# Two of the four weight sums of a seven-product quad made by a copying and an adding transfer on GpSimd's queue, and a sixth such quad in each pass of the ssm branch

## The chip, the cores and the metric

One core of a Trainium2 chip runs one launch of the kernel. The metric is the device time of that launch in microseconds. Timed runs of the kernel before gave 1389.09, 1389.74 and 1391.64, median 1389.74.

## The reference, cut to what matters

One layer of a hybrid block, on 256 rows of width 2048, all in float32: a normed input is projected into queries, keys, values, gates and the inputs of a state-space scan; attention and scan run beside each other; then

```python
merged = sigmoid(g_a) * (o_a @ w_attn_branch) + sigmoid(g_s) * (y @ w_ssm_branch)
x + merged @ w_out
```

and a last norm. The change lies in the product `y @ w_ssm_branch` (256 x 4096 by 4096 x 2048), and touches the products for the gate `g_a` and the values `v` (256 x 2048 by 2048 x 2048 each).

## The kernel before, in words

A float32 product is made of three products of TensorE in a faster format: every operand is split into a high part (ScalarE copies it with rounding, `hq`) and a low part (VectorE subtracts, `lq`), and high by high, high by low and low by high are added up in PSUM.

**Quads.** The branch, gate, value and output products run in passes over 1024 of the 2048 output columns (`quads`, called with `cc` 0 and 1). The unit of a pass is a quad: two blocks of 128 rows of the weight by two halves of 512 columns, so four pieces of 128 x 512, which `lay_quads` lays in DRAM in the order b12, b11, b22, b21 (first figure: the column half). The program holds one quad as two tiles `wq_0` (b12, b11) and `wq_1` (b22, b21), of 512 KB each. An ssm pass has 16 quads, a pass for `ga` or `v` has 8. A plain quad is eight products of a 128 x 128 block by a 128 x 512 piece, 24 matmuls. A quad named in `lefts` is done in seven products by Strassen's scheme (Winograd's form), 21 matmuls, but these need four sums of pieces of weights, and their splits: b11+b12 and b12+b22 (the two halves of the tile `t13`), then b11+b12+b22 and b11+b12+b22+b21 (the tile `t24`), each built on one before it. PE does the products in the order 1, 2, 3, 7, 5, 6, 4 (L786 to L792); 7 and 5 take the split of `t13`, 6 and 4 that of `t24`.

**Where the sums come from.** For `ga`, `v`, attention's branch and the output most seven-product quads have sums that were made earlier and stored in DRAM (`stored`), and load them as `tq`. Sums in line (the `elif seven` in `quad`, from L744) are made for five quads in each of the two ssm passes (1, 3, 5, 7, 9) and for quad 4 in each of the four `ga` and `v` passes: 14 quads, with four VectorE adds each (L751).

**Queues and order.** All weights are loaded by SyncE's queue (L724, L728). A loaded tile takes the next slot of a ring of six (`ring("w")`: four slots of the pool `stream`, two of `more`); its load waits until all readers of the slot's old tile are done. Rings of six also hold the `h` and `l` splits, which come free when PE has used them. `t13` and `t24` had a ring of two of their own (tag `T`). Splits and sums are issued with high priority, and `in_turn` keeps all splits and sums of weights in program order on VectorE. VectorE thus stands still if the next in that order isn't ready. `order` in the call of `quads` gives the order of the quads in a pass; in both ssm passes a seven-product quad stands beside a plain one through most of the pass. GpSimd has little to do: it clears small tiles and, at the start of ssm, makes `r_y` (L381).

Of the kernel before, what the change touches and what calls it, by code (L numbers as in the profile page):

```python
# [9 lines left out]
F32 = mybir.dt.float32  # L10
F32R = mybir.dt.float32r
AF = mybir.ActivationFunctionType
ALU = mybir.AluOpType
PSUM = bass.MemoryType.PSUM

P = 128
# [5 lines left out]
SH = 64  # L22
EPS = 1e-6
KT = D // P
UNIT = 1024
# [97 lines left out]
N_PK = 16 + 4 * 48 + 48 + 32 + 32 + 2  # L123
# [40 lines left out]
def hybrid_block(ctx: ExitStack, tc: tile.TileContext, wall, wq, xt, x, pk_d, cst_d, fw_d, out):  # L164
    nc = tc.nc
    ve, ac, gp, pe = nc.vector, nc.scalar, nc.gpsimd, nc.tensor

    lead = ctx.enter_context(tc.tile_pool(name="lead", bufs=1))
# [12 lines left out]
        return opened.enter_context(tc.tile_pool(name=name, bufs=2))  # L181


    pk = lead.tile([P, N_PK], F32, name="pk", tag="pk")
    half = lead.tile([P, 2], F32, name="half", tag="half")
    a_neg = lead.tile([SH, 1], F32, name="a_neg", tag="a_neg")
    cw = lead.tile([P, 240], F32, name="cw", tag="cw")
    small = lead.tile([P, 8], F32, name="small", tag="small")
    ones2, sums_x = small[:, 0:2], small[:, 2:4]
# [12 lines left out]
    def ring(tag, name):  # L202
        n = W_BUFS if tag == "w" else H_BUFS
        shape, dt = [P, UNIT], F32 if tag == "w" else F32R
        if more is not None:
            turns[tag] += 1
            turn = (turns[tag] - 1) % (n + MORE + (2 if tag == "w" and wide else 0))
            if turn >= n + MORE:
                return summed.tile(shape, dt, name=name, tag="T", bufs=2)
            if turn >= n:  # L210
                return more.tile(shape, dt, name=name, tag=tag, bufs=MORE)
        return stream.tile(shape, dt, name=name, tag=tag, bufs=n)
# [187 lines left out]
    yT0 = big.tile([P, KT, 2 * S], F32R, name="yT0", tag="yo0")  # L400
    yT1 = []
# [29 lines left out]
    def load_on(u):  # L431
        if u < 6:
            load(u + 4)
        if u < 3:
            nc.sync.dma_start(xr(2 * u + 10, 2 * u + 12), xt[:, 2 * u + 10 : 2 * u + 12, :])
        if u == 3:
            nc.sync.dma_start(pk[:, KT:], pk_d[:, KT:])
        if u == 6:

            for late in (th_s[:, 0, 0:1], cst[:, 0:1]):  # L440
                gp.tensor_copy(late, yT0[:, 13, 0:1].bitcast(F32))
            nc.sync.dma_start(th_s, x.rearrange("(i p) d -> p i d", p=P))
            nc.sync.dma_start(cst, cst_d[:, 768:])
# [275 lines left out]
    def quad(n, seven):  # L719
        ws, ts = [], []  # L720
        for j in range(2):
            ws.append(ring("w", f"wq{n}_{j}"))
            cut = 512 if j == 0 and n in stored else 0
            nc.sync.dma_start(ws[j][:, cut:], wq[n, :, j * UNIT + cut : (j + 1) * UNIT])  # L724
        if n in stored:
            for j in range(2):
                ts.append(ring("w", f"tq{n}_{j}"))
                nc.sync.dma_start(ts[j], stored[n][:, j * UNIT : (j + 1) * UNIT])  # L728
        parts = {}

        def halves(src, names, cut=0):
            h, l = ring("h", f"hq{n}_{names[1]}"), ring("l", f"lq{n}_{names[1]}")
            in_turn("h", ac.activation(h[:, cut:], src[:, cut:], AF.Copy))  # L733
            in_turn("l", ve.tensor_tensor(l[:, cut:], src[:, cut:], h[:, cut:].bitcast(F32), ALU.subtract))  # L734
            for j, name in enumerate(names):
                parts[name] = h[:, j * 512 : j * 512 + 512], l[:, j * 512 : j * 512 + 512]

        with tc.high_priority(L_AHEAD):
            halves(ws[0], ("12", "11"), 512 if seven else 0)
            halves(ws[1], ("22", "21"))  # L740
            if ts:
                halves(ts[0], (7, 5))
                halves(ts[1], (6, 4))
            elif seven:  # L744
                b12, b11, b22, b21 = (w[:, c : c + 512] for w in ws for c in (0, 512))
                t13, t24 = (summed.tile([P, UNIT], F32, name=f"t{n}_{e}", tag="T", bufs=2) for e in range(2))
                for t, a, b in (
                    (t13[:, :512], b12, b11), (t13[:, 512:], b12, b22),
                    (t24[:, :512], t13[:, :512], b22), (t24[:, 512:], t24[:, :512], b21),
                ):  # L750
                    in_turn("l", ve.tensor_tensor(t, a, b, ALU.add))  # L751
                halves(t13, (5, 7))
                halves(t24, (6, 4))
        return parts
# [62 lines left out]
    summed = ctx.enter_context(tc.tile_pool(name="summed", bufs=2))  # L817
# [6 lines left out]
    with tc.tile_pool(name="mid", bufs=2) as mid:  # L824
        def two(name):
            return [mid.tile([P, UNIT], F32, name=f"{name}_{e}", tag=f"s{e}", bufs=1) for e in range(2)]

        def norm_y():
            tot = bank("m2", 2, "tot_y")
            for i in range(2):  # L830
                for n in range(2):
                    pe.matmul(
                        tot[:, 2 * i : 2 * i + 2], ssq[:, n, i * P : (i + 1) * P], ones2,
                        start=(n == 0), stop=(n == 1),
                    )
            rsqrt_rows(tot[:, 0:4:2], INNER, "y")

        def scale_gs(cc, i):
            g, r = th_s[:, i, cc * 1024 : (cc + 1) * 1024], hrs[:, 1, i : i + 1]
            ac.activation(g, g, AF.Identity, scale=r, bias=r)  # L840

        sf = mid.tile([P, 5, 2, 3, P], F32R, name="sf_y", tag="sf", bufs=1)
        lefts = {}
        for m, n in enumerate((4, 1)):
            s6 = sf[:, 4 * m : 4 * m + n]
            h3, l3 = s6[:, :, 0], s6[:, :, 1]
            y = yT1[0] if m else yT0
            v = y.rearrange("p (n r) c -> p n r c", r=4)[:, :n, 2]
            h4, l4 = v[:, :, P:S], v[:, :, S + P :]
            left(lambda: two("left"), y, 0, n, h3, l3, h4, l4)  # L850
            for j in range(n):
                lefts[8 * m + 2 * j + 1] = [(h3[:, j, e], l3[:, j, e]) for e in range(3)] + [(h4[:, j], l4[:, j])]

        def gated(i, c, a, b, op):
            g = th_s[:, i, c * 512 : (c + 1) * 512]
            ve.tensor_tensor(b, a, b, op)
            ve.tensor_tensor(g, g, b, ALU.mult)

        def ssm_sums(cc):
            return [[t[:, c * 512 : (c + 1) * 512] for c in range(2)] for t in two(f"sums{cc}")]  # L860

        lefts_x = {}

        def left_x():
            sf = big.tile([P, 5, 2, 4, P], F32R, name="sf_x", tag="yo0")
            h4, l4 = sf[:, :, 0], sf[:, :, 1]
            for j0, n, r, o in ((0, 2, 2, 0), (2, 2, 2, 2), (2, 1, 0, 4)):
                h, l = h4[:, o : o + n], l4[:, o : o + n]
                left(lambda: two("left"), XT, j0, n, h[:, :, :3], l[:, :, :3], h[:, :, 3], l[:, :, 3], r)
            for j, u in enumerate((1, 3, 5, 7, 4)):  # L870
                lefts_x[u] = [(h4[:, j, e], l4[:, j, e]) for e in range(4)]

        for cc, order, then in (
            (0, (0, 2, 4, 6, 1, 8, 3, 10, 5, 12, 7, 11, 9, 13, 14, 15), {1: norm_y, 9: (0, 0), 11: (0, 1)}),
            (1, (1, 0, 3, 2, 5, 4, 7, 6, 8, 10, 11, 12, 9, 13, 14, 15), {2: (1, 0), 4: (1, 1), 7: left_x}),
        ):
            then = {n: f if callable(f) else lambda f=f: scale_gs(*f) for n, f in then.items()}
            quads(
                "ssm", cc, yT, 2 * KT, order, lefts, lambda: ssm_sums(cc), gated, then
            )  # L880

        th_a, vt = (
            [big.tile([P, D], F32, name=f"{n}{i}", tag=f"yo1{2 * e + i}") for i in range(2)]
            for e, n in enumerate(("th_a", "vt"))
        )
        lefts = lefts_x

        def gate(i, c, a, b, op):
            ve.tensor_tensor(b, a, b, op)
            ac.activation(b, b, AF.Tanh, scale=0.5)  # L890

        def value(i, c, a, b, op):
            ve.tensor_tensor(b, a, b, op)

        for tag, dst, finish in (("ga", th_a, gate), ("v", vt, value)):
            for cc in range(2):
                order = (0, 1, 3, 2, 4, 5, 7, 6)
                sums = [[dst[i][:, (2 * cc + c) * 512 : (2 * cc + c + 1) * 512] for c in range(2)] for i in range(2)]
                quads(tag, cc, lambda kt: XT[:, kt, :], KT, order, lefts, lambda: sums, finish)

    with tc.tile_pool(name="att", bufs=2) as ap, tc.tile_pool(name="ev2", bufs=2) as ev, tc.tile_pool(name="odd2", bufs=2) as odd:
# [46 lines left out]
        for h in range(NH):  # L948
# [5 lines left out]
            p = ap.tile([P, 384], F32, name=f"p{h}", tag="p", bufs=2)  # L954
# [11 lines left out]
    with tc.tile_pool(name="fin", bufs=2) as fp:  # L966
# [72 lines left out]
        lefts = empty()  # L1039
# [10 lines left out]
        lefts = empty()  # L1050
# [54 lines left out]
```

## Time and profile before

| what | value |
|---|---|
| timed runs, median | 1389.74 us |
| profiled execution | 1389.4 us |
| its span in the trace | 1387.6 us (1.8 us lie around it) |
| TensorE busy | 1374.8 us, 99% |
| VectorE busy | 1170.2 us, 84% |
| ScalarE busy | 830.5 us, 60% |
| GpSimd busy | 15.5 us, 1% |
| moved by DMA | 356.06 MB, 257 GB/s in the mean |
| ssm passes | 585.16 to 753.4 us |
| `ga` and `v` passes | 753.4 to 913.9 us |

A row of a timeline has the start, the duration, the engine, the line and the operation with its output and inputs; "x3" merges that many in a row. Matmul durations overlap, so what one costs is the step from start to start. The chain of waits is followed back from the last instruction and shows at each time what the rest waited for. "Issue to landing" of a DMA runs from its issue on the queue to its completion.

### The profile page before, as it was taken

The page shows a single profiled execution, that of the slowest core. Times are in us where ns is not written, and L with a number is a line of the kernel's source. Part 1 is how long each engine was busy: PE and PEld are TensorE (multiplying, and loading weights), DVE is VectorE, ACT ScalarE, POOL GpSimd, SP SyncE. Part 2 cuts the span into 40 slices and gives each one's busy share as a digit, 9 for nine tenths or more (in the row PEclk, how much of TensorE's full clock was granted, in tenths as well). Part 3 has the DMA queues.
Part 4 walks back from the last instruction along what each step waited for, and adds up shares of the span by engine and source line. Part 5 has one row for each costly group of instructions (what it writes and reads, how often), then busy time and mean ns, then how long its engine had stood idle before and what let it go on. Part 6 is the DMA issues. An engine that isn't in the chain of part 4 may idle for free.

```text
span 1387.6 us, 20439 instructions
## 1 busy us (share of the span) xinstructions
PE 1374.8 (99%) x7275; PEld 1170.2 (84%) x7275; DVE 1170.2 (84%) x1746; ACT 830.5 (60%) x1278; POOL 15.5 (1%) x70
## 2 busy tenths in 40 slices
PE   9999999999999999999999999999999999999997
PEld 7888888888888888888888888888888888878885
DVE  6988899887898888699997888887778776677997
ACT  6657767757566757465454667554544454464564
POOL 0000000000000000000000000000000000000010
PEclk9999999999999999999999999999999999999998
DMA  8678888798878775557576888898888887468765
GB/s 336 212 213 286 269 296 269 258 327 270 283 262 285 233 243 183 180 185 241 173 234 205 292 285 284 281 317 301 302 294 291 285 288 229 150 243 303 281 209 185
DMA packets 103110, 356.06 MB, mean 257 GB/s; under 512 B 11552, under 2 KB 12128, under 8 KB 102368
## 3 DMA queue, kind: packets, MB, share of 16 engines
q1 hardware_dynamic: 102432, 353.71, 75.9%
q8 instruction: 57, 0.93, 0.3%
q10 hardware_dynamic: 576, 1.05, 0.2%
q14 instruction: 45, 0.37, 0.1%
HBM read 322.14 MB, written 32.57 MB: 256 GB/s over the span
## 4 chain that ended last, share of the span: by engine, by line
PE 93%; DMA 3%; DVE 2%; ACT 1%; issue 1%; SPq 0%; POOL 0%; POOLq 0%; DVEq 0%; ACTq 0%
PE ps_xs L303 8%; PE ps_zs L303 8%; PE ps_xs L306 4%; PE ps_zs L306 4%; PE ps_q L303 4%; PE ps_k L303 4%; PE ps_za L303 4%; PE ps_ssm L771 4%; PE ps_ssm L772 4%; PE ps_ssm L773 4%; PE ps_k L306 2%; PE ps_za L306 2%; PE ps_q L306 2%; PE ps_gs L369 2%; PE ps_gs L368 2%; PE ps_gs L367 2%
## 5 line engine op out<-in xcount | busy, mean ns | idle before, releaser
L236 ACT ACTIVATE h<-w 128x1024 fp32r<-128x1024 f32 (+1 forms) x293 | 306.3, 1047 | 279.1 <-PE ps_za L303 47.5
L237 DVE TENSOR_TENSOR l<-w,h 128x1024 fp32r<-128x1024 f32 (+1 forms) x293 | 352.6, 1206 | 101.9 <-ACT h L236 99.1
L734 DVE TENSOR_TENSOR lq<-wq,hq 128x512 fp32r<-128x512 f32 (+1 forms) x192 | 206.6, 1100 | 43.6 <-ACT hq L733 42.5
L733 ACT ACTIVATE hq<-wq 128x512 fp32r<-128x512 f32 (+1 forms) x192 | 179.1, 959 | 105.6 <-PE ps_attn L773 16.2
L303 PE MATMUL ps_xs<-XT,h 128*128 128x512 f32 x496 | 176.3, 396 | 0.0
L303 PE MATMUL ps_zs<-XT,h 128*128 128x512 f32 x496 | 175.4, 395 | 0.0
L306 PE MATMUL ps_xs<-XT,l 128*128 128x256 f32 x496 | 139.7, 282 | 0.0
L306 PE MATMUL ps_zs<-XT,l 128*128 128x256 f32 x496 | 139.2, 281 | 0.0
L303 PEld LDWEIGHTS ps_xs<-XT,h 128*128 128x128 f32 x496 | 93.1, 188 | 21.1
L303 PEld LDWEIGHTS ps_zs<-XT,h 128*128 128x128 f32 x496 | 93.0, 187 | 21.1
L306 PEld LDWEIGHTS ps_xs<-XT,l 128*128 128x128 f32 x496 | 93.6, 189 | 0.8 <-issue 0.3
L306 PEld LDWEIGHTS ps_zs<-XT,l 128*128 128x128 f32 x496 | 93.6, 189 | 0.3
L303 PE MATMUL ps_q<-XT,h 128*128 128x512 f32 x256 | 90.6, 393 | 0.0
L303 PE MATMUL ps_za<-XT,h 128*128 128x512 f32 x256 | 89.7, 392 | 0.0
L303 PE MATMUL ps_k<-XT,h 128*128 128x512 f32 x256 | 89.7, 392 | 0.0
L772 PE MATMUL ps_ssm<-lq,yT 128*128 128x512 f32 x216 | 83.9, 389 | 0.0
L773 PE MATMUL ps_ssm<-hq,yT 128*128 128x512 f32 x216 | 83.7, 389 | 0.0
L733 ACT ACTIVATE hq<-tq 128x1024 fp32r<-128x1024 f32 x58 | 60.2, 1053 | 31.9 <-DMA tq<-sums_d 12.7
L734 DVE TENSOR_TENSOR lq<-tq,hq 128x1024 fp32r<-128x1024 f32 x58 | 69.2, 1218 | 11.9 <-ACT hq L733 11.9
L771 PE MATMUL ps_ssm<-hq,yT 128*128 128x512 f32 x216 | 77.1, 390 | 0.0
L306 PE MATMUL ps_q<-XT,l 128*128 128x256 f32 x256 | 74.4, 291 | 0.0
L306 PE MATMUL ps_k<-XT,l 128*128 128x256 f32 x256 | 71.7, 280 | 0.0
(325 smaller groups left out, 3001.9 us busy)
## 6 DMA issues: line engine op xcount, KB each, us to landing
w<-in_wall SPq DMA_DIRECT2D x288, 512.0 KB, 5.4
wq<-in_wq SPq DMA_DIRECT2D x163, 512.0 KB, 4.9
st<-in_wq SPq DMA_DIRECT2D x58, 512.0 KB, 5.1
sums_d<-st SPq DMA_DIRECT2D x58, 512.0 KB, 6.0
tq<-sums_d SPq DMA_DIRECT2D x58, 512.0 KB, 5.7
acb<-acum_d SPq DMA_DIRECT2D x32, 256.0 KB, 3.9
wq<-in_wq SPq DMA_DIRECT2D x29, 256.0 KB, 4.7
th_s<-in_x SPq DMA_DIRECT2D x1, 2048.0 KB, 10.0
```

The lines of the kernel that those rows point to most:

```text
L236: ac.activation(h[:, a:b], w[:, a:b], AF.Copy)
L237: last = ve.tensor_tensor(l[:, a:b], w[:, a:b], h[:, a:b].bitcast(F32), ALU.subtract)
L303: pe.matmul(acc[:width], h[:, kk, :], m, start=(kt == 0), stop=False)
L306: pe.matmul(acc[:width, S:], l[:, kk, :], m[:, :S], start=False, stop=(kt == n_kt - 1))
L367: pe.matmul(accs[i], xh, h, start=(kt == 0), stop=False)
L368: pe.matmul(accs[i], xh, l, start=False, stop=False)
L369: pe.matmul(accs[i], xl, h, start=False, stop=(kt == n_kt - 1))
L733: in_turn("h", ac.activation(h[:, cut:], src[:, cut:], AF.Copy))
L734: in_turn("l", ve.tensor_tensor(l[:, cut:], src[:, cut:], h[:, cut:].bitcast(F32), ALU.subtract))
L771: pe.matmul(accs[b], x[0], w[0], start=first, stop=False)
L772: pe.matmul(accs[b], x[0], w[1], start=False, stop=False)
L773: pe.matmul(accs[b], x[1], w[0], start=False, stop=stop)
```

## The change

In the branch without stored sums, `t13` is no longer made by VectorE. It takes a slot of the ring of six that the loaded weights use. GpSimd's queue first copies b12 from DRAM into both halves of it (one transfer of 512 KB written, 256 KB of DRAM read twice), and then adds b11 and b22 from DRAM onto it in a second transfer (512 KB). The second waits for the first. `t24` stays on VectorE with two adds; the first reads `t13` and b22, the second b21. All 16 quads with sums in line (there are 14 before) are made so.

In both ssm passes quad 11 becomes a seven-product quad, with its left factors made from the second of the `yT1` tiles; the order of the last quads is changed so that 9 and 11 stand between plain ones. To make room, the 64 numbers `a_neg` become a column of `pk`.

```diff
-    a_neg = lead.tile([SH, 1], F32, name="a_neg", tag="a_neg")
+    a_neg = pk[:SH, N_PK:]
...
-                b12, b11, b22, b21 = (w[:, c : c + 512] for w in ws for c in (0, 512))
-                t13, t24 = (summed.tile([P, UNIT], F32, name=f"t{n}_{e}", tag="T", bufs=2) for e in range(2))
+                b22, b21 = ws[1][:, :512], ws[1][:, 512:]
+                t13 = ring("w", f"t{n}_0")
+                gp.dma_start(
+                    t13.rearrange("p (a c) -> p a c", a=2), wq[n, :, :512].unsqueeze(1).to_broadcast([P, 2, 512])
+                )
+                gp.dma_start(t13, wq[n, :, 512 : 512 + UNIT], accum_op=ALU.add)
+                t24 = summed.tile([P, UNIT], F32, name=f"t{n}_1", tag="T", bufs=2)
                 for t, a, b in (
-                    (t13[:, :512], b12, b11), (t13[:, 512:], b12, b22),
                     (t24[:, :512], t13[:, :512], b22), (t24[:, 512:], t24[:, :512], b21),
                 ):
                     in_turn("l", ve.tensor_tensor(t, a, b, ALU.add))
...
-        sf = mid.tile([P, 5, 2, 3, P], F32R, name="sf_y", tag="sf", bufs=1)
+        sf = mid.tile([P, 6, 2, 3, P], F32R, name="sf_y", tag="sf", bufs=1)
...
-        for m, n in enumerate((4, 1)):
+        for m, (y, n) in enumerate(((yT0, 4), (yT1[0], 1), (yT1[1], 1))):
...
-            (0, (0, 2, 4, 6, 1, 8, 3, 10, 5, 12, 7, 11, 9, 13, 14, 15), {1: norm_y, 9: (0, 0), 11: (0, 1)}),
-            (1, (1, 0, 3, 2, 5, 4, 7, 6, 8, 10, 11, 12, 9, 13, 14, 15), {2: (1, 0), 4: (1, 1), 7: left_x}),
+            (0, (0, 2, 4, 6, 1, 8, 3, 10, 5, 12, 7, 13, 9, 14, 11, 15), {1: norm_y, 9: (0, 0), 11: (0, 1)}),
+            (1, (1, 0, 3, 2, 5, 4, 7, 6, 8, 10, 9, 12, 11, 13, 14, 15), {2: (1, 0), 4: (1, 1), 7: left_x}),
```

GpSimd's instructions at the start of the ssm passes, before (`raw_x` are the last cleared tiles of the scan, `r_y` is the norm's factor, `fs` belongs to the end of the kernel):

```order
L516 MEMSET raw_x_5913 128x4
L516 MEMSET raw_x_6042 128x4
L381 TENSOR_TENSOR r_y<-var_y,half 128x2
L1031 TENSOR_TENSOR fs<-fs 128x1
L1032 TENSOR_SCALAR fs<-fs 128x1
```

The same place now (`t_0_6539` is `t13` of the ssm pass's quad 1, `t_0_6626` that of quad 3):

```order
L516 MEMSET raw_x_6041 128x4
L747 DMA t_0_6539<-in_wq 128x2x512
L381 TENSOR_TENSOR r_y<-var_y,half 128x2
L750 DMA t_0_6539<-in_wq 128x1024
L747 DMA t_0_6626<-in_wq 128x2x512
L750 DMA t_0_6626<-in_wq 128x1024
```

A queue that was empty from `r_y` to the end now holds 32 transfers, in pairs; `r_y` stands between the first two.

VectorE in the first ssm pass, before: a plain quad (12), then a seven-product quad (7) with its four sums (`lq` are low parts, `t_0` is `t13`, `t_1` is `t24`):

```order
L734 TENSOR_TENSOR lq_11_6739<-wq_0_6734,hq_11_6738 128x1024
L734 TENSOR_TENSOR lq_21_6743<-wq_1_6736,hq_21_6742 128x1024
L734 TENSOR_TENSOR lq_11_6776<-wq_0_6771,hq_11_6775 128x512
L734 TENSOR_TENSOR lq_21_6780<-wq_1_6773,hq_21_6779 128x1024
L751 TENSOR_TENSOR t_0_6783<-wq_0_6771 128x512
L751 TENSOR_TENSOR t_0_6783<-wq_0_6771,wq_1_6773 128x512
L751 TENSOR_TENSOR t_1_6784<-t_0_6783,wq_1_6773 128x512
L751 TENSOR_TENSOR t_1_6784<-t_1_6784,wq_1_6773 128x512
L734 TENSOR_TENSOR lq_7_6790<-t_0_6783,hq_7_6789 128x1024
L734 TENSOR_TENSOR lq_4_6794<-t_1_6784,hq_4_6793 128x1024
```

The same two quads now:

```order
L734 TENSOR_TENSOR lq_11_6749<-wq_0_6744,hq_11_6748 128x1024
L734 TENSOR_TENSOR lq_21_6753<-wq_1_6746,hq_21_6752 128x1024
L734 TENSOR_TENSOR lq_11_6786<-wq_0_6781,hq_11_6785 128x512
L734 TENSOR_TENSOR lq_21_6790<-wq_1_6783,hq_21_6789 128x1024
L755 TENSOR_TENSOR t_1_6796<-t_0_6793,wq_1_6783 128x512
L755 TENSOR_TENSOR t_1_6796<-t_1_6796,wq_1_6783 128x512
L734 TENSOR_TENSOR lq_7_6800<-t_0_6793,hq_7_6799 128x1024
L734 TENSOR_TENSOR lq_4_6804<-t_1_6796,hq_4_6803 128x1024
```

Two of the four sums are gone from VectorE; the first of the two that stay reads what GpSimd's transfers have written.

More of the change, by code (lines that the diff above doesn't have):

```diff
@@ L181, in pool @@
         return opened.enter_context(tc.tile_pool(name=name, bufs=2))
-    pk = lead.tile([P, N_PK], F32, name="pk", tag="pk")
+    pk = lead.tile([P, N_PK + 1], F32, name="pk", tag="pk")
     half = lead.tile([P, 2], F32, name="half", tag="half")
-    a_neg = lead.tile([SH, 1], F32, name="a_neg", tag="a_neg")
+    a_neg = pk[:SH, N_PK:]
     cw = lead.tile([P, 240], F32, name="cw", tag="cw")
@@ L436, in load_on @@
         if u == 3:
-            nc.sync.dma_start(pk[:, KT:], pk_d[:, KT:])
+            nc.sync.dma_start(pk[:, KT:N_PK], pk_d[:, KT:])
         if u == 6:
@@ L840, in scale_gs @@
             ac.activation(g, g, AF.Identity, scale=r, bias=r)
-        sf = mid.tile([P, 5, 2, 3, P], F32R, name="sf_y", tag="sf", bufs=1)
+        sf = mid.tile([P, 6, 2, 3, P], F32R, name="sf_y", tag="sf", bufs=1)
         lefts = {}
-        for m, n in enumerate((4, 1)):
-            s6 = sf[:, 4 * m : 4 * m + n]
+        for m, (y, n) in enumerate(((yT0, 4), (yT1[0], 1), (yT1[1], 1))):
+            s6 = sf[:, 3 + m : 4 + m] if m else sf[:, :4]
             h3, l3 = s6[:, :, 0], s6[:, :, 1]
-            y = yT1[0] if m else yT0
             v = y.rearrange("p (n r) c -> p n r c", r=4)[:, :n, 2]
@@ L851, in hybrid_block @@
             for j in range(n):
-                lefts[8 * m + 2 * j + 1] = [(h3[:, j, e], l3[:, j, e]) for e in range(3)] + [(h4[:, j], l4[:, j])]
+                lefts[2 * (3 + m if m else j) + 1] = [(h3[:, j, e], l3[:, j, e]) for e in range(3)] + [(h4[:, j], l4[:, j])]
         def gated(i, c, a, b, op):
```

## The prediction

> **What bounds the kernel now.** I read the page's first part, then who waited for whom on PE, then busy time by stage.
>
> ```profile
> span 1387.6 us, 20439 instructions
> PE 1374.8 (99%) x7275; PEld 1170.2 (84%) x7275; DVE 1170.2 (84%) x1746; ACT 830.5 (60%) x1278; POOL 15.5 (1%) x70
> ...
> PE warm L418 <- POOL ssq L415: 1.4, 1, 1.4
> PE ps_first L327 <- ACT h L236: 1.2, 2, 1.0
> PE ps_attn L771 <- ACT hq L733: 0.4, 1, 0.4
> PE ps_v L771 <- ACT hq L733: 0.2, 1, 0.2
> ```
>
> TensorE is the bound. Its four waits in the whole kernel add up to 3.2 us, and only the last, 0.2 us, lies in what the change touches. So there is hardly a stall to win; time goes down only with the number of matmuls, and goes up as soon as something is late for PE. By stage (ssm passes, then `ga` and `v`; the columns used are PE, DVE, and at the end clock, DMA share and GB/s):
>
> ```profile
> 585.16:753.40 168.24, 168.24 (x746) 139.41 (x747) 154.13 (x200) 93.43 (x109) 1.61 (x1) 1.00 0.63 205
> 753.40:913.90 160.50, 160.34 (x708) 132.49 (x707) 138.02 (x148) 105.11 (x116) 0.00 (x0) 1.00 0.84 287
> ...
> 610.00:651.00 41.00, 41.00 (x182) 33.91 (x181) 39.99 (x50) 25.25 (x29) 0.00 (x0) 1.00 0.65 207
> ```
>
> In ssm PE is never idle and the granted clock is 1.00, but VectorE is close behind: 154 of 168 us, and 39.99 of 41 us where seven-product and plain quads alternate. DMA has room there (0.63, 205 GB/s) and less in `ga` and `v` (0.84, 287 GB/s).
>
> **Part 1: the sixth seven-product quad.** The chain of waits shows what a matmul costs when PE runs through:
>
> ```profile
> 690.62 0.45 PE ps_ssm L771 x2
> 692.43 0.91 PE ps_ssm L771 x4
> ```
>
> 0.91 / 4 = 0.227 us. Two quads (one a pass) go from 24 matmuls to 21: 6 x 0.227 = **-1.36 us**, all on the path, since PE has no idle time there. A plain quad then takes 24 x 0.227 = 5.44 us on PE, one of seven products 4.76, a pair of both 10.2. The added splits and left factors go to ScalarE (93 of 168 us busy) and VectorE.
>
> **Part 2: VectorE's load.** The sums before, one quad of the first pass, and the splits between two quads' sums:
>
> ```profile
> 625.61 0.68 DVE L751 TENSOR_TENSOR t<-wq 128x512 f32<-128x512 f32 x1
> 626.21 0.68 DVE L751 TENSOR_TENSOR t<-wq,wq 128x512 f32<-128x512 f32 x1
> 626.82 1.41 DVE L751 TENSOR_TENSOR t<-t,wq 128x512 f32<-128x512 f32 x2
> 628.14 2.52 DVE L734 TENSOR_TENSOR lq<-t,hq 128x1024 fp32r<-128x1024 f32 x2
> 630.58 4.09 DVE L734 TENSOR_TENSOR lq<-wq,hq 128x1024 fp32r<-128x1024 f32 x4
> 634.58 0.68 DVE L751 TENSOR_TENSOR t<-wq 128x512 f32<-128x512 f32 x1
> ```
>
> A pair takes 634.58 - 625.61 = 8.97 us of VectorE. The two adds that go are the first two rows, 626.82 - 625.61 = 1.21 us, so a pair takes 7.8 us, against PE's 10.2. For the two new quads VectorE does, against a plain quad, two more splits and two adds less half a split, 2.4 + 1.3 - 0.5 = 3.2 us, and some 1.5 us of left factors; the ten older ones give back 12.1. Net about -3 us on VectorE in ssm: no loss, and no gain either, since PE never waited for it.
>
> **Part 3: the two transfers, on which all hangs.** `t13` is now late or in time by GpSimd's queue. In a run of pairs five slots are taken by each pair, and the slot that `t13` of one seven-product quad takes is six places back: the tile `wq_1` of the seven-product quad before. That is read last by the second add of that quad's `t24`. So from one `t24` to the next lies one chain: end of the add, copy (D1), adding transfer (D2), two adds (1.3 us by the step of the row "x2" above), and signals between them (0.15, a guess from the 0.05 us steps of "issue" in the chain below). With D = D1 + D2, the period is L = D + 1.45. PE needs one quad every 10.2 us. While VectorE waits for `t13`, its later splits wait too, by `in_turn`.
>
> How much may L exceed 10.2? The first seven-product quad:
>
> ```profile
> 605.53 0.68 DVE L751 TENSOR_TENSOR t<-t,wq 128x512 f32<-128x512 f32 x1
> ...
> 609.97 0.62 PE L771 MATMUL ps_ssm<-hq,sf_y 128*128 128x512 f32 x2
> ...
> 598.47 1.61 POOL L381 TENSOR_TENSOR r_y<-var_y,half 128x2 f32<-128x2 f32 x1 [50.03 <-DVE var_y L379]
> ```
>
> PE came to product 7 at 609.97. Its low part is used 0.23 us later and takes VectorE about 1.0 after the sums, so they must be done by 609.2. They were, at 606.2. Now D2 is queued behind `r_y` on GpSimd, which ends at 600.1; with 4.5 to 6 us and two adds the sums end at 605.9 to 607.4. The lead at the start is thus 1.8 to 3.3 us; I take 2.5. Ten such quads follow each other without a break (1, 3, 5, 7, 9, 11 and, in the second pass, 1, 3, 5, 7), so nine periods: no stall if 9 x (L - 10.2) < 2.5, that is L < 10.48, **D < 9.0 us**. Above that every 1 us of D costs 9 us.
>
> No transfer on GpSimd's queue, and none that adds, is in the trace. The nearest rows are SyncE's 512 KB loads, first in the ssm passes:
>
> ```profile
> L724 SPq DMA_DIRECT2D wq<-in_wq x63: 327/328/425, 584.8 to 745.6; - x63
> ...
> DMA to landing us min/median/max: 3.4/4.5/6.9
> ...
> wq<-in_wq SPq DMA_DIRECT2D x2, 256.0 KB, 4.0
> ...
> wq<-in_wq SPq DMA_DIRECT2D x44, 512.0 KB, 5.5
> tq<-sums_d SPq DMA_DIRECT2D x28, 512.0 KB, 5.8
> ```
>
> The first four rows are of the ssm passes, the last two of `ga` and `v`. Two transfers in series: 6.8 us by the least, 9.0 by the median, 13.8 by the most. I take D1 = 4.0 (only 256 KB come out of DRAM, and nothing stands before it in its own queue, where SyncE's loads come in twos) and D2 = 4.5 to 5.0 (it reads its target as well): D = 8.5 to 9.0, just at the bound. Stall 0 at 8.5.
>
> The Trainium skill, in "DMA: Bandwidth & Descriptors", section "Anatomy of one DMA — SWDGE (gpsimd) path", fits 2.0 us plus bytes over 436 GB/s for a transfer of that queue: 3.2 us for 512 KB as an estimate, 6.4 for both. By that the sum is -1.36 with 2.6 us to spare; no run here shows a transfer of that kind yet, and by the rows above there is nearly nothing to spare.
>
> **Part 4: the four `ga` and `v` passes.** They get the transfers too, one pair a pass. The last pass is the tight one; the chain of waits there:
>
> ```profile
> 881.82 6.03 DMA wq<-in_wq
> 887.91 0.05 issue
> 887.96 1.07 ACT hq L733
> 889.05 1.23 DVE lq L734
> 890.27 1.82 DVE t L751 x3
> 892.12 0.70 DVE t L751
> ...
> 895.88 8.11 DMA tq<-sums_d
> 904.09 1.07 ACT hq L733
> 905.20 0.73 PE ps_v L771 x2
> ```
>
> It runs from a slot that comes free at 881.8 through quad 4's load and its sums to the next load and PE's 0.2 us wait. `t13` would take the slot of quad 3's first stored sum, whose split ends one split later, about 882.9. With D = 8.5 it has landed at 891.5, VectorE's two adds end at 892.8, as now. Each us more of D is a us of stall there. The `a_neg` column, the two new left factors' ScalarE work (at 56% busy) and `r_y`, whose readers come quads later, I cost at nothing: none stands before a matmul that waits.
>
> **The sum.** -1.36 us at D up to 8.5. The profiled execution took 1389.4, so 1388.0; on the median of the runs, 1389.74, it is **1388.4 us**. A change of 0.2%, 2.8 us, is about what a measurement of this kernel can tell from none, so this is no change that can be told.
>
> **The rivals.**
>
> A. *The chain over `t13` becomes the bound* (slower). Mechanism: D above 9.0, so PE waits in each of the pairs after the lead is used. For it: the ssm passes get 12 x 1.05 MB more over 168 us, 75 GB/s, so 280 in all, nearly the 287 at which the loads of `ga` and `v` take 5.5 us. Two of those are 11.0: L = 12.45, stall 9 x 2.25 - 2.5 = 17.8 us, time 1389.7 - 1.4 + 17.8 = 1406. With D = 10.3 (one at 4.5, one at 5.8) it is L = 11.75, 11.4 us, 1399.8. Against it: those 5.5 us hold waiting behind up to three other loads of the same queue, which GpSimd's does not have. It is slower by 0.2% from D = 9.5 on (L = 10.95, 9 x 0.75 - 2.5 = 4.3, less 1.36). The skill's section "Issuing engines are not separate DMA queues" on the same page says that transfers of all queues run on the same 16 engines and interleave; by it the added 75 GB/s would lengthen all loads and this rival is the likelier one.
>
> B. *ssm keeps up, the last `v` pass doesn't.* At 5.5 us each D = 11.0 there, the adds end at 882.9 + 11.0 + 1.45 = 895.4, 2.6 us later than now: 1391.0. The three passes before have about 1 us more lead, so little more comes from them. Still within 0.2%.
>
> C. *VectorE's relief brings more than the matmuls*, faster. It would need idle time of PE to remove; there is 0.2 us in these stages. To pass 2.8 us, over 1.4 would have to come from elsewhere, and I see no place.
>
> D. *The change doesn't do what it says*: the sixth quads save nothing since their factors or sums are late. The left factors are made in the first four quads, 22 us ahead of PE's first use; what is late then is A at a small D. 1389.7 to 1391.
>
> **How the numbers follow.** Forecast 0.38, B 0.09, D 0.04: no change, 0.51. A: 0.47, since D's rows reach from 6.8 to 13.8 around a bound of 9.0. C: 0.02. The likeliest one's own range is 1387.6 to 1389.7. The range asked for must go into A: to 1407, past its 5.5-us-loads case, which leaves about 0.1 above; at the lower end 1387.2, -1.36 with another 1.2 us, leaves 0.04.
>
> **What would show it.** Right: 738 matmuls on `ps_ssm` become 732, still at 0.227; no wait of PE in the ssm passes; on VectorE the step from one quad's first `t24` add to the next stays 10.2 us or less; D1 + D2 below 9.0 from issue to landing. A: that step is 11 us and more, VectorE idle before the first `t24` add with the transfer as releaser, and PE waiting for ScalarE's `hq` in pairs from about the third seven-product quad on. B: the first wait of PE in the last `v` pass. Wrong altogether: transfers of under 7 us for both and still a loss, which would mean contention on other loads, not the chain.

## The result, and the profile after

The changed kernel takes **1491.68 us** in the median of four runs (1487.79 to 1494.25), against 1390.07 us for four runs of the kernel before beside it: a ratio of 1.0727, 95% interval 1.0715 to 1.0740. It is about 100 us slower. The forecast was 1388.4 with a range to 1407, so both were wrong; of the rivals it is A, at several times its price.

The first part of the page, then PE's waits (total us, times, longest):

```profile
span 1486.0 us, 20553 instructions
...
PE 1414.6 (95%) x7269; PEld 1190.1 (80%) x7269; DVE 1161.1 (78%) x1733; ACT 831.5 (56%) x1284; POOL 41.6 (3%) x102
...
PEclk9999999999999999978899999999999999999999
...
DMA t<-in_wq 10%; PE ps_xs L303 8%; PE ps_zs L303 8%; PE ps_xs L306 4%; PE ps_zs L306 4%; PE ps_q L303 4%; PE ps_za L303 4%; PE ps_k L303 4%; DMA tq<-sums_d 2%; PE ps_k L306 2%; PE ps_za L306 2%; PE ps_q L306 2%; PE ps_gs L369 2%; PE ps_gs 
```

```profile
PE ps_ssm L775 <- ACT hq L733: 41.5, 20, 5.3
PE ps_v L775 <- ACT hq L733: 8.6, 5, 3.9
PE ps_ga L775 <- ACT hq L733: 7.3, 4, 3.0
```

PE has the six matmuls less that were forecast (7275 before, 7269 now). But PE, which had 0.2 us of waits in these stages, now has 57. The releaser named is ScalarE's `hq`; ScalarE is not the cause, since the same page has the transfers into `t13` (`t<-in_wq`) as the first item of the chain that ended last, and in its groups ScalarE and VectorE both wait for them:

```profile
L733 ACT ACTIVATE hq<-t 128x1024 fp32r<-128x1024 f32 x32 | 33.8, 1058 | 156.4 <-DMA t<-in_wq 146.0
L755 DVE TENSOR_TENSOR t<-t,wq 128x512 f32<-128x512 f32 x32 | 22.1, 691 | 115.9 <-DMA t<-in_wq 115.5
```

By stage (ssm, the two `ga` passes, the two `v` passes; PE, PEld, DVE, ACT, POOL busy, granted clock, DMA share, GB/s):

```profile
585.00:825.00 240.00, 197.00 (x740) 152.75 (x741) 149.98 (x195) 96.59 (x115) 21.29 (x25) 0.86 0.68 195
825.00:916.30 91.30, 84.02 (x348) 67.85 (x347) 64.87 (x69) 50.94 (x58) 3.22 (x4) 0.94 0.80 265
916.30:1012.40 96.10, 87.54 (x365) 70.39 (x364) 68.04 (x74) 52.91 (x60) 3.21 (x4) 0.95 0.83 277
```

The ssm passes went from 168.2 to 240.0 us (+72), `ga` and `v` together from 160.5 to 187.4 (+27). That is the whole difference of the spans, 98.4 us. The ssm stage moves fewer GB/s than before (195 against 205), though its DMA engines are busy a larger share of it (0.68 against 0.63). That this is not a lack of bandwidth is shown further on, by number 9, which moves 250 GB/s in the same stage without loss.

One period of the chain of waits in ssm, from one first `t24` add to the next (start, us, what; "issue" at 648.07 is the copy on its way, which the chain doesn't name):

```profile
645.23 0.70 DVE t L755
645.93 0.03 issue
645.96 0.70 DVE t L755
646.65 0.03 POOLq L747
646.69 0.65 issue
647.34 0.73 POOL t L747
648.07 5.34 issue
653.41 0.01 POOLq L747
653.42 8.46 DMA t<-in_wq
661.88 0.03 issue
661.91 0.02 DVEq L755
661.93 0.04 issue
661.98 0.70 DVE t L755
```

There is no PE in it, so PE doesn't set this pace. Two adds 1.4, 0.7 from the last add to the copy's issue, copy 6.1, adding transfer 8.5, 0.1 to the next add: 16.75 us. PE needs a quad of this kind every 10.2. The two transfers over the whole kernel, copy first:

```profile
DMA to landing us min/median/max: 4.6/6.2/8.0
DMA to landing us min/median/max: 6.5/7.6/9.2
```

VectorE's `t24` adds of the first, the fourth and the tenth seven-product quad:

```profile
610.92 1.42 DVE L755 TENSOR_TENSOR t<-t,wq 128x512 f32<-128x512 f32 x2 [6.62 <-DMA t<-in_wq]
661.98 1.42 DVE L755 TENSOR_TENSOR t<-t,wq 128x512 f32<-128x512 f32 x2 [8.90 <-DMA t<-in_wq]
762.76 1.42 DVE L755 TENSOR_TENSOR t<-t,wq 128x512 f32<-128x512 f32 x2 [8.11 <-DMA t<-in_wq]
```

(762.76 - 610.92) / 9 = 16.87 us a period, and each time VectorE stands idle 6.6 to 8.9 us for the transfer.

### The profile page after: what moved, and what is told of

It reads as the page before. It is cut to its first block, busy times and chain, and to the rows that moved or that the text cites. A ratio compares the mean times of both kernels' runs of the same rounds, so it can differ in the third digit from the quotient of the medians.

```text
span 1486.0 us, 20553 instructions
## 1 busy us (share of the span) xinstructions
PE 1414.6 (95%) x7269; PEld 1190.1 (80%) x7269; DVE 1161.1 (78%) x1733; ACT 831.5 (56%) x1284; POOL 41.6 (3%) x102
## 4 chain that ended last, share of the span: by engine, by line
PE 74%; DMA 13%; issue 7%; DVE 3%; ACT 1%; POOL 1%; SPq 0%; POOLq 0%; DVEq 0%; ACTq 0%
DMA t<-in_wq 10%; PE ps_xs L303 8%; PE ps_zs L303 8%; PE ps_xs L306 4%; PE ps_zs L306 4%; PE ps_q L303 4%; PE ps_za L303 4%; PE ps_k L303 4%; DMA tq<-sums_d 2%; PE ps_k L306 2%; PE ps_za L306 2%; PE ps_q L306 2%; PE ps_gs L369 2%; PE ps_gs L368 2%; PE ps_gs L367 2%
## 5 line engine op out<-in xcount | busy, mean ns | idle before, releaser
L733 ACT ACTIVATE hq<-t 128x1024 fp32r<-128x1024 f32 x32 | 33.8, 1058 | 156.4 <-DMA t<-in_wq 146.0
L755 DVE TENSOR_TENSOR t<-t,wq 128x512 f32<-128x512 f32 x32 | 22.1, 691 | 115.9 <-DMA t<-in_wq 115.5
L734 DVE TENSOR_TENSOR lq<-tq,hq 128x1024 fp32r<-128x1024 f32 x58 | 69.6, 1222 | 12.9 <-ACT hq L733 12.8
```

## The experiments

The theory: *the chain*. `t13` takes a slot that the quad before gives back only after its `t24` adds, so both transfers lie in series between one quad's adds and the next's. Its rivals: *traffic*, the transfers make all loads slower; *the sixth quads*, whose work VectorE or ScalarE can't carry; *the adding* itself, being slow; and *the ring*, in which `t13` takes one of the six slots that the loads had. Each ratio is against runs of the kernel before on the same chip.

**1. The sixth quads alone.** The changed kernel with the four VectorE sums of before:

```diff
-                t13 = ring("w", f"t{n}_0")
-                gp.dma_start(
...
-                gp.dma_start(t13, wq[n, :, 512 : 512 + UNIT], accum_op=ALU.add)
...
+                t13, t24 = (summed.tile([P, UNIT], F32, name=f"t{n}_{e}", tag="T", bufs=2) for e in range(2))
+                    (t13[:, :512], b12, b11), (t13[:, 512:], b12, b22),
```

> The sixth seven-product quad alone: all four sums on VectorE as before, no transfer on GpSimd's queue. Theory (the chain copy, adding transfer, sums, slot makes the whole loss): two quads save 6 x 0.227 = 1.36 us and VectorE's 8.97 us a pair stay under TensorE's 10.2, so 1388.7 us, within 1387.5 to 1390. Rival (the sixth quad costs by itself, by VectorE or by a worse order of the last quads): 1393 to 1420.

Measured 1393.64, ratio 1.003 (1.0021 to 1.0039): 4 us slower, the rival's number. After the new quad VectorE (the third busy time) has hardly a gap, and PE has a wait that the kernel before doesn't have, for an `hq` that stands behind VectorE's sums:

```profile
672.00:712.00 40.00, 37.75 (x160) 30.59 (x159) 39.78 (x49) 20.51 (x23) 0.00 (x0) 0.96 0.54 173
```

```profile
PE ps_ssm L771 <- ACT hq L733: 2.8, 2, 2.3
```

The sixth quads explain 4 of the 100 us. But VectorE's relief is not worthless, as I had it: without it the sixth quad costs more than its matmuls save. (The new order and the left factors are not what costs: number 4 has them too, with two VectorE adds a quad less, and loses nothing.)

**2. The transfers alone.** The kernel before, five quads a pass, with the changed branch for `t13`:

```diff
-                t13, t24 = (summed.tile([P, UNIT], F32, name=f"t{n}_{e}", tag="T", bufs=2) for e in range(2))
+                t13 = ring("w", f"t{n}_0")
+                gp.dma_start(
...
+                gp.dma_start(t13, wq[n, :, 512 : 512 + UNIT], accum_op=ALU.add)
...
-                    (t13[:, :512], b12, b11), (t13[:, 512:], b12, b22),
```

> The transfers alone: five seven-product quads a pass as before, t13 made by copy and adding transfer. Chain theory: a period of 16.9 us against TensorE's 10.2, but the run of quads is broken by three plain quads (13, 14, 15) between the passes, where 21 us pass between two seven-product quads: 4 x 6.7 - 2.5 = 24 us in the first pass, 3 x 6.7 - 4 = 16 in the second, and about 25 in the ga and v passes as after: near 1455 us. Rival (traffic on the 16 DMA engines): the loss goes with the number of transfers, 28 of 32, +88 us, 1478. Rival (the sixth quads): back to 1390.

Measured 1469.23, 1.0573 (1.0559 to 1.0587). The transfers are the cause, sixth quads are not needed for it. The number lies between chain and traffic (1455 and 1478) and doesn't separate them. The trace does: the `t24` adds of the five quads of the first pass go from 611.93 to 680.34, (680.34 - 611.93) / 4 = 17.1 us a period, each after an idle time of VectorE that ends with the transfer.

**3. The slot taken earlier.** `t13` takes its slot and starts its transfers ahead of its own quad's loads:

```diff
+        if seven and n not in stored:
+            t13 = ring("w", f"t{n}_0")
+            gp.dma_start(
...
+            gp.dma_start(t13, wq[n, :, 512 : 512 + UNIT], accum_op=ALU.add)
...
             elif seven:
-                t13 = ring("w", f"t{n}_0")
-                gp.dma_start(
...
-                gp.dma_start(t13, wq[n, :, 512 : 512 + UNIT], accum_op=ALU.add)
```

> As the changed kernel, but t13 takes its slot of the ring ahead of the quad's two loads, and both transfers are issued there. Same bytes, same transfers, same number of slots. Its slot then is that of the plain quad before the seven-product quad in front, so the chain closes over two pairs only: 15.2 of transfers + 1.3 of adds + 4.2 of splits = 20.7 us for 20.4 of TensorE. Chain theory: the ssm passes lose 0 to 8 us instead of 72, the ga and v passes about 3 us less each than after: 1395 to 1420 us. Rival (traffic on the DMA engines, or too few slots for the loads): as after, 1480 to 1495.

Measured 1437.55, 1.0346 (1.0332 to 1.0360), outside both ranges. The same bytes and transfers cost half as much when only the place of the slot and of the issue changes: this speaks for the chain and against traffic. The `t24` adds of the first seven seven-product quads go from 606.91 to 683.93, (683.93 - 606.91) / 6 = 12.8 us a period, still above 10.2. Now the loads are late too (ScalarE's waits for `wq` are 62.1 us, 12.1 in the kernel before):

```profile
ACT hq L739 <- DMA wq<-in_wq: 62.1, 43, 6.9
ACT hq L739 <- DMA t<-in_wq: 38.1, 10, 5.5
```

A slot held from the start of the copy to the last read is missing for the loads. So it seems to be not only which slot `t13` gets, but also how long one of the loads' six is held; this is read from the waits, no run varies it by itself.

**4. The copy alone.**

```diff
-                gp.dma_start(t13, wq[n, :, 512 : 512 + UNIT], accum_op=ALU.add)
```

> As the changed kernel without the adding transfer (t13 holds b12 twice, so the sums are not those of the reference). Chain theory: period 0.7 + 6.1 + 1.5 = 8.3 us, below 10.2, so no stall in ssm and next to none in ga and v: 1388 to 1392 us. Rival (traffic): half the added bytes are left, half the loss, about 1440 us.

Measured 1391.37, 1.0007 (0.9998 to 1.0016): the loss is gone, with the slot's place as in the changed kernel and half of D. The copies take 4.7 / 7.2 / 8.0 us (least, median, most), so L is about 7.2 + 2.2 = 9.4, below 10.2. PE's waits on `ps_ssm` are 0.7 us, the stage takes 168.6 us (168.2 before):

```profile
584.70:753.30 168.60, 167.86 (x743) 138.22 (x741) 149.60 (x196) 97.51 (x115) 10.57 (x13) 1.00 0.73 242
```

`t13` still takes one of the six slots here, and the slot is still the shared one. So neither the ring with a slot less nor the shared slot costs anything by itself; what costs is a loop that takes longer than 10.2 us.

**5. A plain second transfer.** The second transfer overwrites instead of adding.

```diff
-                gp.dma_start(t13, wq[n, :, 512 : 512 + UNIT], accum_op=ALU.add)
+                gp.dma_start(t13, wq[n, :, 512 : 512 + UNIT])
```

> As the changed kernel, but the second transfer copies b11 and b22 over t13 instead of adding them (the sums are not those of the reference). The same two transfers in series. Chain theory: the loss goes with the period. If adding costs nothing beside copying, the second transfer stays at 7.6 us and the time at 1491; if it costs the difference to the copy of b12 (7.6 against 6.2), the period falls from 16.9 to 15.5, 13 to 18 us less: near 1475. Rival (the adding itself is the cause): back to 1390.

Measured 1460.01, 1.0500 (1.0481 to 1.0519). The second transfer now takes 4.9 / 6.0 / 7.6 us: adding costs 1.6 us by the medians. The gain, 31 us, is above the 13 to 18 expected: the period falls by 2.0 us, to (744.43 - 610.96) / 9 = 14.83, a little more than the 1.6, and `ga` and `v` gain too. 70 of the 100 us stay with two plain transfers in series, so the adding makes it worse and isn't the cause.

**6. The transfers, unread, in the kernel before.** Every seven-product quad also makes a copying and an adding transfer of 376 KB into a tile that nobody reads; nothing waits for them.

```diff
+                idle = idles[0]
+                gp.dma_start(idle.rearrange("p (a c) -> p a c", a=2), wq[n, :, :376].unsqueeze(1).to_broadcast([P, 2, 376]))
+                gp.dma_start(idle, wq[n, :, 512 : 512 + 752], accum_op=ALU.add)
```

> The kernel before, with its sums on VectorE and five seven-product quads, and beside it 28 transfers in pairs on GpSimd's queue, a copy and an adding transfer of 376 KB written each, into a tile that nobody reads (73% of the change's bytes, and issued one pair behind the other). Chain theory: nobody waits, so 1390 to 1393 us; the loads get longer by up to 1 us each. Rival (traffic on the 16 engines, or GpSimd's descriptor work against VectorE): 50 us or more, 1440 and up.

Measured 1413.23, 1.0163 (1.0144 to 1.0183), neither of the two. The ssm passes are as before (168.2 us, no wait of PE). Nearly all the rest is one wait of 18.7 us at the start of `ga`. The chain of waits there:

```profile
777.71 5.00 DMA idle<-in_wq
783.05 0.33 SPq L908
783.38 0.05 issue
783.48 0.38 SPq L724
```

The load of the masks (L908) at the head of SyncE's queue takes over memory of the unread tile, waits for the last unread transfer, and the weight loads (L724) stand behind it. That is a fault of the experiment; number 9 repeats it without.

**7. Slots of its own.** Six quads, both transfers; `t13` gets back its ring of two, and `t24` is made in place over `wq_1`:

```diff
-                t13 = ring("w", f"t{n}_0")
+                t13 = summed.tile([P, UNIT], F32, name=f"t{n}_0", tag="T", bufs=2)
...
-                t24 = summed.tile([P, UNIT], F32, name=f"t{n}_1", tag="T", bufs=2)
+                t24 = ws[1]
...
-                    (t24[:, :512], t13[:, :512], b22), (t24[:, 512:], t24[:, :512], b21),
+                    (b22, t13[:, :512], b22), (b21, b22, b21),
```

> As the changed kernel, six seven-product quads and both transfers, but t13 has the ring of two of its own (tag T) and t24 is made in place over wq_1, so that the loads keep all six slots. A slot of t13 then comes free two seven-product quads (20.4 us) ahead, and the transfers, 13.8 us, fit. Chain theory: no stall in ssm, the sixth quads save 1.36 us: 1388 to 1391. Rival (traffic): 1430 to 1490 as in the runs before.

Measured 1405.91, 1.0106 (1.0091 to 1.0122). The same bytes, the same transfers, the same products: 86 of the 102 us are gone. Traffic can't have made them. The edit opens the chain and also gives the loads their sixth slot back; that the chain is what counts follows from this run and number 4 together. Some 16 us stay, which I had not expected. GpSimd's queue, an adding transfer (L750) and the next quad's copy (L747) behind it:

```profile
644.22 0.87 POOL L750 DMA_DIRECT2D t<-in_wq  x1 [8.72 <-DMA t<-in_wq]
644.87 0.97 POOL L747 DMA_DIRECT2D t<-in_wq  x1
656.00 0.90 POOL L750 DMA_DIRECT2D t<-in_wq  x1 [10.16 <-DMA t<-in_wq]
656.65 1.00 POOL L747 DMA_DIRECT2D t<-in_wq  x1
667.62 0.87 POOL L750 DMA_DIRECT2D t<-in_wq  x1 [9.97 <-DMA t<-in_wq]
```

The copy now goes out right behind an adding transfer, lands only 10 to 11 us later, and the queue gives one pair per 11.7 us (667.62 - 644.22 over 2). In the stage DMA is 0.90 busy at 276 GB/s.

**8. The same with five quads a pass.** The kernel before, with the branch of number 7:

```diff
-                t13, t24 = (summed.tile([P, UNIT], F32, name=f"t{n}_{e}", tag="T", bufs=2) for e in range(2))
+                t13 = summed.tile([P, UNIT], F32, name=f"t{n}_0", tag="T", bufs=2)
...
+                t24 = ws[1]
...
+                    (b22, t13[:, :512], b22), (b21, b22, b21),
```

> As e7_own_slots with five seven-product quads a pass and the order of the kernel before. Chain theory: 1.36 us above e7_own_slots, the same as before: 1389.5 to 1391. If VectorE's relief is worth something by itself it is below before.

Measured 1402.32, 1.0082 (1.0067 to 1.0097): 3.6 us *below* number 7, where 1.36 above was expected (the intervals just overlap). With a limit of 11 to 12 us per quad one more quad of this kind wouldn't pay; that this is the reason was not tested.

**9. Unread transfers, ssm only.** As number 6, for the ten ssm quads alone:

```diff
+                idle = idles[0]
+                if n < QFIRST["ga", 0]:
...
+                  gp.dma_start(idle, wq[n, :, 512 : 512 + 752], accum_op=ALU.add)
```

> As e6_unread_transfers, but with the 20 unread transfers of the ten ssm quads alone (the others delayed one load of SyncE's queue there, the attention masks', that takes over their tile's memory). Chain theory: PE has no wait in ssm and the time is that of before, 1389 to 1392 us. Rival (traffic on the 16 engines slows the kernel by itself): 1400 and more.

Measured 1390.93, 1.0007 (0.9997 to 1.0016). The ssm stage:

```profile
585.70:753.80 168.10, 168.10 (x745) 138.93 (x744) 153.41 (x200) 93.52 (x108) 18.11 (x21) 1.00 0.80 250
```

250 GB/s instead of 205, loads at 5.5 us instead of 4.5, PE never idle, clock 1.00. **Transfers of three quarters of the size, for ten of twelve quads, cost nothing** that can be told; the rival falls for transfers that nobody waits for.

**10. ScalarE copies.** With slots of its own, b12 goes into `t13` by a ScalarE copy, and one adding transfer follows.

```diff
-                gp.dma_start(
-                    t13.rearrange("p (a c) -> p a c", a=2), wq[n, :, :512].unsqueeze(1).to_broadcast([P, 2, 512])
+                ac.activation(
+                    t13.rearrange("p (a c) -> p a c", a=2), ws[0][:, :512].unsqueeze(1).to_broadcast([P, 2, 512]), AF.Copy
```

> As e7_own_slots, but ScalarE copies b12 into both halves of t13 from the loaded tile, and GpSimd's queue has the adding transfer alone. Theory (in e7_own_slots the two transfers of a pair, 10 and 1.7 us, and so 11.5 us a pair on GpSimd's queue, are the bound): one transfer of some 8 us is below 10.2, so the queue keeps up; ScalarE has 1.05 us more a quad. 1388 to 1394. Rival (adding transfer behind ScalarE's copy comes too late, since the copy waits for the quad's own load): 1400 to 1430.

Measured 1416.34, 1.0191 (1.0175 to 1.0207). ScalarE's waits:

```profile
ACT hq L733 <- DMA t<-in_wq: 41.4, 14, 6.5
ACT t L747 <- DMA wq<-in_wq: 40.6, 14, 4.2
```

The copy has to wait for the quad's own load, which a transfer from DRAM doesn't, and the adding transfer comes after that. Removing a transfer is of no use if what replaces it starts later.

**11. GpSimd computes.** With slots of its own, GpSimd makes the two `t13` sums as adds instead of transfers.

```diff
-                gp.dma_start(t13, wq[n, :, 512 : 512 + UNIT], accum_op=ALU.add)
+                gp.tensor_tensor(t13[:, :512], ws[0][:, :512], ws[0][:, 512:], ALU.add)
+                gp.tensor_tensor(t13[:, 512:], ws[0][:, :512], b22, ALU.add)
```

> As e7_own_slots, but GpSimd computes the two sums of t13 itself from the loaded tiles, with no transfer. No chain over a slot and no traffic; what is open is GpSimd's speed on 128 x 512 sums, which no run shows. At up to 2 us each they lie beside VectorE's splits: 1388 to 1392. If a sum takes 4 us and more, or holds VectorE up, slower than before: 1395 to 1430.

Measured 1403.89, 1.0095 (1.0080 to 1.0110). `ga` and `v` are back at 159.8 us. The ssm stage:

```profile
585.30:766.10 180.80, 171.39 (x740) 138.10 (x739) 169.31 (x195) 96.52 (x114) 57.68 (x25) 0.99 0.57 190
```

VectorE is busy 169 us there, in number 7 it was 150 with the same 195 instructions: its splits of 128x1024 take 1.37 us in the mean, against 1.22. So VectorE gets slower while GpSimd works; that this makes the whole loss was not tested. One of GpSimd's adds is recorded with 13.0 us (at 685.47), and PE's longest wait of the stage, 3.9 us, ends right behind it.

**12. The copy on SyncE's queue.** As number 7, the copy issued by SyncE:

```diff
-                gp.dma_start(
+                nc.sync.dma_start(
```

> As e7_own_slots, with the copy issued on SyncE's queue and only the adding transfer on GpSimd's. Same bytes. Theory (GpSimd's queue, whose copy lies behind the adding transfer of the quad before, sets the pace of 11.5 us a pair): 1389 to 1396. Rival (the bytes): as e7_own_slots, 1403 to 1409, or worse since the loads now queue behind the copies.

Measured 1399.42, 1.0073 (1.0057 to 1.0090), between the two. The copies take 3.8 / 5.9 / 7.5 us there (7.5 in the median in number 7), and some 6 of the 16 us go (1405.91 - 1390.24 = 15.7 in number 7, 1399.42 - 1389.96 = 9.5 here; the intervals just miss each other). The sums of the first seven quads now come every (669.87 - 609.32) / 6 = 10.1 us, so that share was the pace of GpSimd's queue. The other 10 stay open; the adding transfers take 6.9 / 8.9 / 10.3 and DMA is 0.91 busy at 284 GB/s, which no run here varied by itself. No version beat the kernel before.

## Why the prediction was wrong, point by point

**The failing step is in Part 3: "D = 8.5 to 9.0, just at the bound".** The chain, the order of its links and its ten quads were right; the term put into it was mis-sized. Measured are 6.2 for D1 instead of 4.0 and 7.6 for D2 instead of 4.5 to 5.0: D = 13.8 by the medians of all, the most that the quoted rows allowed (twice 6.9), and 16.87 - 2.2 = 14.7 in the ten periods. D1 was set below the median of the nearest 512 KB rows for two reasons that the runs don't bear out. The first was that only half the bytes come out of DRAM. The page's line on DRAM ("HBM"), of the kernel before and of number 4, which adds 16 copies and no other transfer:

```profile
HBM read 322.14 MB, written 32.57 MB: 256 GB/s over the span
```

```profile
HBM read 330.53 MB, written 32.57 MB: 262 GB/s over the span
```

8.39 MB for 16 copies is 512 KB each: the 256 KB are read twice, so the copy is as large a transfer as a load. The second was that nothing stands ahead of it in its queue; that was so in the loop, and the copy took 6.2 all the same. D2 was given half a microsecond for the adding; number 5 measures 1.6. And the signals add up to 0.8 us a period, most of it the 0.7 from the last add to the copy's issue, where the guess was 0.15.

The Trainium skill's fit in "DMA: Bandwidth & Descriptors", section "Anatomy of one DMA — SWDGE (gpsimd) path", 3.2 us for 512 KB as an estimate, disagrees with every such transfer in the changed kernel: the least of the copies took 4.6, of the adding ones 6.5.

**The formula with the measured terms.** The period of 16.87 gives 9 x (16.87 - 10.2) = 60.0 us. The lead of 2.5, and with it the bound of 9.0 for D, was wrong: it was a lag. GpSimd at the first seven-product quad, in the changed kernel:

```profile
597.14 0.95 POOL L747 DMA_DIRECT2D t<-in_wq  x1 [48.92 <-PE tot_y L836]
598.13 1.62 POOL L381 TENSOR_TENSOR r_y<-var_y,half 128x2 f32<-128x2 f32 x1
604.00 0.92 POOL L750 DMA_DIRECT2D t<-in_wq  x1 [4.24 <-DMA t<-in_wq]
```

I had the adding transfer wait for `r_y` alone, until 600.1; it waited for the copy, until 604.0, so the first sums ended at 612.3, 3.1 us after the 609.2 at which they were needed, and PE waited (2.2 us) at the first of the ten quads already, not from the third on. Quads 9 and 11 of the second pass, which I had left out as not in a row, add 8.1: from the tenth adds at 762.76 to the last at 802.16 are 39.4 us, in which PE has 4.76 + 3 x 5.44 + 10.2 = 31.3 of work. 60.0 + 3.1 + 8.1 - 1.4 = 69.8 of the 72 us found.

**Part 1** was right in the count (six matmuls) and in 0.227 us for each while the clock is full. The 1.36 us were never seen: where the chain is cured (number 4), the ssm stage takes as long as before.

**Part 2** had VectorE's load about right (154.1 us in ssm before, 150.0 now; -4.2, with -3 forecast). It was wrong in "no gain": with five quads PE never waited, but number 1 shows that six don't fit on VectorE without the relief.

**Part 4** had the rule, "each us more of D is a us of stall", but priced it for the last pass alone and left about 1 us of lead to the three before. From the copy's issue to the end of the adding transfer the four pairs take 13.0 to 14.6, 14.0 in the mean, instead of 8.5, and all four passes lose: 4 x 5.5 = 22 us by the rule, 27 found.

**Rivals.** A had the mechanism, shown by numbers 4, 5, 7 and 9 together: the same bytes without the shared slot (7) lose 16 us instead of 102, three quarters of the size without a reader (9) or one transfer in the same slot (4) lose nothing, and the ssm stage follows the period of the loop (240.0 us at 16.87, 215.8 at 14.83 in number 5, 168.6 in number 4, where the loop is below 10.2). It had a chance of 0.47, and should have been the forecast: of the three ends quoted for two transfers, 6.8, 9.0 and 13.8, the bound stood at the median, and both unknowns (another queue, and an adding transfer) pointed upwards. Its price stopped at two 5.5 us loads; D = 13.8 gives L = 15.25 and 9 x 5.05 - 2.5 = 43 us, so the range left out an end that the text itself had named. The Trainium skill's section "Issuing engines are not separate DMA queues" in "DMA: Bandwidth & Descriptors", that transfers of all queues run on the same 16 engines and interleave, was cited for A. The loads did lengthen (4.5 to 5.5 in number 9), but this alone cost nothing. B is contained in the result; C and D did not happen. "Wrong altogether", contention without the chain, is excluded by number 9 as the main cause in ssm, at 250 GB/s; for the 10 us that stay in number 12, at 284 GB/s, it stays open.

## What to carry to other kernels

Before a compute step is handed to transfers, draw the loop from the slot's last reader round to the next reader: all that lies in it in series must fit into one period of the engine that bounds, and a slot taken from the ring of the loads closes such a loop. Price a transfer on a queue that the trace has not shown at the far end of the nearest rows, and two in series at twice that; where the bound lies in the middle of the ends, as here, give the slow case more weight than the fast one. Transfers of three quarters of the size that nobody waited for cost nothing in ssm; the full ones in a loop cost 72 us there.

## What the runs showed of the hardware

After such a wait of PE the granted clock is halved for some microseconds (0.50 from 645 to 650 us, 1.00 again from 651.7). PE in the changed kernel, first at the wait of the period shown above, then behind it:

```profile
646.35 1.22 PE L775 MATMUL ps_ssm<-hq,sf_y 128*128 128x512 f32 x2 [3.79 <-ACT hq L733]
...
648.89 0.63 PE L776 MATMUL ps_ssm<-lq,sf_y 128*128 128x512 f32 x1
649.32 0.63 PE L777 MATMUL ps_ssm<-hq,sf_y 128*128 128x512 f32 x1
649.75 0.63 PE L776 MATMUL ps_ssm<-lq,sf_y 128*128 128x512 f32 x1
...
651.94 0.39 PE L777 MATMUL ps_ssm<-hq,sf_y 128*128 128x512 f32 x1
652.16 0.40 PE L776 MATMUL ps_ssm<-lq,yT 128*128 128x512 f32 x1
```

The step is 0.43 us until 651.7 and 0.23 after it. That is why PE's recorded waits (57 us) are less than the loss (98): part of a late quad shows as busy time at a lower clock (0.86 in ssm); PE's busy time grew by 39.8 us, from 1374.8 to 1414.6, with six matmuls less. In ssm the chain sets the period whatever the clock, so there it hides; in `ga` and `v`, where 16 us of waits stand against 27 lost, it may add.

The adding transfer took 1.6 us more than a plain one of the same size and place (7.6 against 6.0), and kept GpSimd busy 0.88 us to issue instead of 0.57. What it takes depends on the kernel around it too: 6.1 in the median in number 10, 8.9 in number 12. A copy from DRAM into both halves of a tile read DRAM twice. A GpSimd add of 128x512 took 1.8 us on `t13`'s first half and 1.9 on its second in the median (1.3 at the least, one 13.0), and VectorE's 128x1024 splits of loaded tiles took 1.37 us in the mean instead of 1.22 in that kernel.
